# Queries and keys of a streaming-encoder layer: turned by VectorE and DMAs instead of TensorE

## The chip, the cores and the metric

The kernel runs on one core of a Trainium2 chip. The metric is device time in microseconds (us) of one execution; less is better. A core has five engines that run their own instruction queues side by side and wait for each other by semaphores: TensorE (matmuls, PE in the profile), VectorE (DVE), ScalarE (ACT), GpSimd (POOL) and SyncE (SP, which here only issues transfers). Transfers (DMA) are issued from the queues of SyncE, ScalarE and GpSimd. SBUF is the on-chip memory of 128 partitions; PSUM takes TensorE's results.

## The reference

One layer of depth 1 on 256 tokens of width 2048, in float32:

```
x += 1/2 * SwiGLU(RMSNorm(x))
h = RMSNorm(x);  [u | q | k | v] = h @ w_in          # u, q, k, v: 1024 columns each
y_ssm = GLU(S5(u))                                   # diagonal complex state space, scanned in time
q = rms_norm(q, q_norm);  k = rms_norm(k, k_norm)    # per head: 8 heads of 128, gain of 128 numbers
y_sb  = StickBreakingAttention(q, k, v)
x += concat(RMSNorm(y_ssm), RMSNorm(y_sb)) @ w_out
x += 1/2 * SwiGLU(RMSNorm(x))
x += RMSNorm((p @ w_ple_proj) * sigmoid(RMSNorm(x) @ w_ple_gate))
```

For the change the third and fourth lines matter. A head's query is q * rsqrt(mean(q*q) + eps) * q_norm, and the same for a key; the scores are q.k / sqrt(128) for each head. The scores' matmul contracts over the 128 numbers of a head, so both must lie with these numbers along the partitions, while the projection gives them with tokens along the partitions: they have to be turned.

## The kernel before

**Gemms.** Every large product is done in blocks of 512 columns. Weights come in quarters of 4 x 128 rows x 512 columns (1 MB, tile `raw`, three buffers, issued by SyncE). ScalarE casts each half of a quarter to a rounded part `whi` (L168), VectorE subtracts to get the rest `wlo` (L171); four buffers of each. TensorE does three products per tile, activation high x weight high (L292), low x high (L293), high x low (L297), into two of four accumulators `acc` in PSUM. A half quarter is one *step*: 12 matmuls. A cast can begin when the matmuls of four steps before have left its buffer.

**What sets the order.** The program is written as one stream of gemm steps. Other work hangs on it by `put_off(n, fn)`: `fn` is called n steps later, by `step()` after each half quarter. A recording layer then orders each engine's queue by its own costs; instructions that are pinned keep their place. On the chip each engine works its queue strictly in order, so an instruction that waits holds up all that stand behind it.

**The stage around the change.** After the first feed-forward part, `u_block` takes two blocks of u, then come four blocks: queries, keys, queries, keys (`qk_block`, L964), each 512 columns or four heads. Between their steps the state space runs in four groups q (`s5_main`): states (L843), rotation on VectorE (L860, L861), scan (L870), rotation back (L878 to L883), outputs on TensorE (L899), a copy (L919), a Gelu (L930) into `mid`. After the last Gelu `channels` (L945) moves the result into place by 32 small transfers `zt` on SyncE's queue, in between the loads of weights. Then come the blocks of v, the scores (`attn_scores`, L1009 to L1019), the gated unit (`glu`, L1144 to L1170) and the output projection.

**`qk_block` before.** Two scaled copies of the accumulators (L967), one square (L968), a reduction per head on VectorE (L970), a root in `rsqrt_mean` (L188 to L196), a product with it (L972). Five steps later TensorE turns the eight 128x128 pieces (`qk_turn`, L982) into PSUM, and a step after that ScalarE copies them to SBUF, scaled by the norm's gain, which lies along the partitions by then (`qk_scale`, L989).

**Turning by VectorE and DMAs.** Other tiles of the kernel are turned in another way: VectorE transposes the 32x32 blocks (`turn_blocks`, L203), and 16 transfers per tile carry the quarters of 32 partitions to their places (`turn_quarters`, L216).

**Row sums of the unit.** For the norm of y_ssm GpSimd adds the squares (L1090), TensorE sums them over partitions (`rms`, L1074), and a root follows. `glu` puts this off by 3 steps.

## Time and profile before

| | |
|---|---|
| median of 3 runs | 1879.85 us (1879.83 to 1881.18) |
| profiled execution | 1879.88 us |
| its span, first to last instruction | 1878.1 us |
| TensorE busy / VectorE / ScalarE / GpSimd | 1869.5 / 1184.8 / 963.8 / 50.3 us |
| granted TensorE clock | 1.000 |
| blocks of queries and keys, end of each on TensorE | 801.6, 828.5, 854.7, 879.6 us |

The profile gives start and length of instructions in us from the span's start, mean lengths in ns, and for idle time what ended it ("<-"). Matmuls overlap each other, so TensorE's busy time says little; the pitch from one step to the next is what to read. "q" behind an engine (SPq) means its queue, which issues transfers. L numbers are lines of the kernel before.

### The profile page before, as it was taken

What the parts mean: (1) busy time and instruction counts of PE and PEld (TensorE: products, weight loads), DVE (VectorE), ACT (ScalarE), POOL (GpSimd) and SP (SyncE); (2) the same over time, 40 slices, a digit from 0 to 9 for tenths busy, and PEclk for the clock granted to TensorE, in tenths of its full rate; (3) what the DMA queues carried; (4) which work ended last, traced back from release to release, by engine and by line L of the source; (5) the groups of instructions that cost most, each with busy time, mean ns of one, the idle gap of its engine ahead of it and who ended that gap; (6) DMA issues with size and microseconds to landing.
All of it is one profiled execution on the core that took longest, in us unless ns stands there. A gap on an engine that the chain in (4) does not pass through costs nothing.

```text
span 1878.1 us, 23877 instructions
## 1 busy us (share of the span) xinstructions
PE 1869.5 (100%) x9194; PEld 1549.5 (83%) x9194; DVE 1184.8 (63%) x1391; ACT 963.8 (51%) x1110; POOL 50.3 (3%) x84
## 2 busy tenths in 40 slices
PE   9999999999999999999999999999999999999998
PEld 7888888888888888888888888888888888888887
DVE  8867665444676776696566655455545566777655
ACT  7444444444455665455785544444444455666554
POOL 0011000000000000010020000000000000000000
PEclk9999999999999999999999999999999999999999
DMA  8788867766665667675646657666667665666563
GB/s 320 246 274 269 265 209 228 225 211 212 207 204 201 197 212 234 186 263 155 217 136 223 222 186 220 195 209 201 205 201 220 191 222 195 203 211 205 181 235 124
DMA packets 230387, 400.07 MB, mean 213 GB/s; under 512 B 26401, under 2 KB 50337, under 8 KB 229985
## 3 DMA queue, kind: packets, MB, share of 16 engines
q1 hardware_dynamic: 227824, 392.81, 65.2%
q0 software_dynamic: 1728, 4.33, 0.7%
q8 instruction: 72, 1.18, 0.3%
q10 hardware_dynamic: 720, 1.41, 0.2%
q14 instruction: 43, 0.34, 0.1%
HBM read 369.26 MB, written 9.83 MB: 202 GB/s over the span
## 4 chain that ended last, share of the span: by engine, by line
PE 97%; ACT 2%; DMA 0%; POOL 0%; issue 0%; SPq 0%; POOLq 0%
PE acc L292 32%; PE acc L297 32%; PE acc L293 32%; PE aux L899 0%; ACT whi L168 0%; DMA raw<-in_ffn_w_gate 0%; ACT nhi L178 0%; POOL sqg L1090 0%; PE aux L843 0%; PE aux L982 0%; PE aux L716 0%; ACT sg L1161 0%; PE aux L1015 0%; ACT L1161 0%; ACT L1034 0%
## 5 line engine op out<-in xcount | busy, mean ns | idle before, releaser
L171 DVE TENSOR_TENSOR wlo<-raw,whi 128x1024 fp32r<-128x1024 f32 x666 | 811.8, 1225 | 587.0 <-ACT whi L168 579.1
L168 ACT CAST whi<-raw 128x1024 fp32r<-128x1024 f32 x666 | 699.5, 1055 | 835.0 <-PE acc L293 776.2
L292 PE MATMUL acc<-whi,nhi 128*128 128x512 f32 x1568 | 613.5, 391 | 0.8 <-ACT whi L168 0.4
L293 PE MATMUL acc<-whi,nlo 128*128 128x512 f32 x1568 | 610.5, 389 | 0.0
L297 PE MATMUL acc<-wlo,nhi 128*128 128x512 f32 x1568 | 420.7, 389 | 0.0
L292 PE MATMUL acc<-whi,hhi 128*128 128x512 f32 x1056 | 410.8, 389 | 0.0
L293 PE MATMUL acc<-whi,hlo 128*128 128x512 f32 x1056 | 410.8, 389 | 0.0
L292 PEld LDWEIGHTS acc<-whi,nhi 128*128 128x128 f32 x1568 | 294.5, 188 | 63.9 <-ACT whi L260 1.3
L297 PEld LDWEIGHTS acc<-wlo,nhi 128*128 128x128 f32 x1568 | 294.3, 188 | 61.7 <-DVE wlo L171 0.4
L293 PEld LDWEIGHTS acc<-whi,nlo 128*128 128x128 f32 x1568 | 294.6, 188 | 60.3
L297 PE MATMUL acc<-wlo,hhi 128*128 128x512 f32 x1056 | 282.2, 389 | 0.0
L293 PEld LDWEIGHTS acc<-whi,hlo 128*128 128x128 f32 x1056 | 198.3, 188 | 41.2
L297 PEld LDWEIGHTS acc<-wlo,hhi 128*128 128x128 f32 x1056 | 198.2, 188 | 41.1
L292 PEld LDWEIGHTS acc<-whi,hhi 128*128 128x128 f32 x1056 | 198.2, 188 | 41.1
L171 DVE TENSOR_TENSOR hlo<-hT,hhi 128x1024 fp32r<-128x1024 f32 x88 | 107.2, 1219 | 0.0
L168 ACT CAST hhi<-hT 128x1024 fp32r<-128x1024 f32 x88 | 91.6, 1042 | 0.1
L464 DVE SCALAR_TENSOR_TENSOR h<-acc,sm,sg 128x512 f32<-128x512 f32 x44 | 31.0, 747 | 23.7 <-PE acc L297 23.7
L440 ACT ACTIVATE sg<-acc,sm 128x512 f32<-128x512 f32 x44 | 27.7, 681 | 6.8 <-PE acc L297 5.1
L203 DVE STREAM_TRANSPOSE mid<-h 128x512 f32<-128x512 f32 x44 | 28.6, 689 | 0.0
L829 POOL COPY dec<-rho 128x512 f32<-128x512 f32 x8 | 9.6, 1233 | 540.9 <-DVE hlo L171 441.6
L1322 POOL TENSOR_SCALAR sm<-sm,sm 128x1 f32<-128x1 f32 x1 | 0.3, 258 | 881.1 <-DVE sq L1315 881.1
L180 DVE SCALAR_TENSOR_TENSOR nlo<-h,gains,nhi 128x256 fp32r<-128x256 f32 x52 | 22.8, 489 | 1.2 <-ACT nhi L178 1.2
(251 smaller groups left out, 657.5 us busy)
## 6 DMA issues: line engine op xcount, KB each, us to landing
raw<-in_ffn_w_up SPq DMA_DIRECT2D x88, 1024.0 KB, 5.7
raw<-in_ffn_w_down SPq DMA_DIRECT2D x88, 1024.0 KB, 5.1
raw<-in_ffn_w_gate SPq DMA_DIRECT2D x86, 1024.0 KB, 5.2
raw<-in_w_in SPq DMA_DIRECT2D x32, 1024.0 KB, 5.7
raw<-in_w_out SPq DMA_DIRECT2D x16, 1024.0 KB, 5.3
raw<-in_w_ple_gate SPq DMA_DIRECT2D x16, 1024.0 KB, 5.4
hT<-mid SPq DMA_DIRECT2D x160, 64.0 KB, 4.9
h<-mid SPq DMA_DIRECT2D x176, 32.0 KB, 3.7
```

What stands on the lines that cost most here:

```text
L168: copy = nc.scalar.copy(hi, src)
L171: nc.vector.tensor_tensor(out=lo, in0=src, in1=hi.bitcast(F32), op=ALU.subtract)
L180: nc.vector.scalar_tensor_tensor(out=lo[:, j], in0=src[:, j], scalar=scale, in1=hi[:, j].bitcast(F32), op0=ALU.mult, op1=ALU.subtract,)
L203: nc.vector.transpose(mid[:, :, t, k0 : k0 + nk, :].rearrange("p q f b -> p f q b"), src.rearrange("p (f q b) -> p f q b", f=nk, q=4),)
L292: nc.tensor.matmul(ps[t], lhsT=lh, rhs=hi[:, j, cols], start=start and j == 0, stop=False)
L293: nc.tensor.matmul(ps[t], lhsT=ll, rhs=hi[:, j, cols], start=False, stop=False)
L297: nc.tensor.matmul(ps[t], lhsT=lh, rhs=lo[:, j, cols], start=False, stop=stop and j == 1)
L440: nc.scalar.activation(sg[:, t * NB : (t + 1) * NB], pg[t], AF.Silu, scale=xn.rs(t))
L464: nc.vector.scalar_tensor_tensor(out=hh[:, t * NB : (t + 1) * NB], in0=pu[t], scalar=xn.rs(t), in1=sg[:, t * NB : (t + 1) * NB], op0=ALU.m ...
L829: nc.gpsimd.tensor_copy(dvw[:, e], rho4[:, r0 : r0 + 4].unsqueeze(1).unsqueeze(3).to_broadcast([P, 2, 4, NC]))
L1322: pin(nc.gpsimd.tensor_scalar(total, square, 1.0 / D, ahead, op0=ALU.mult, op1=ALU.add))
```

## The change

Queries and keys are kept with tokens along the partitions until all their factors are in. The squares are taken per head straight from the accumulators, with their sums (eight small ones instead of two copies, a square and a reduction); the root is multiplied by the row's factor, eight small copies apply it, and a step later a product with the gain, now laid along the free dimension and loaded by two new transfers (`norms`), follows. Then VectorE turns the 32x32 blocks and 16 transfers on GpSimd's queue carry the quarters into place. TensorE's transposes and the scaled copies out of PSUM are gone. Queries come out in runs of 32 tokens, keys with a step of four numbers between tokens, so the operands of the scores are no longer contiguous. The first load of the kernel is two columns narrower. The row sums of the unit are put off by 4 steps instead of 3.

```diff
-    def turn_quarters(out, mid, steps):
+    def turn_quarters(out, mid, steps, queue=nc.sync):
...
-                    nc.sync.dma_start(
+                    queue.dma_start(
                         out[32 * q : 32 * q + 32].rearrange("p (t i w) -> p t i w", t=TT, i=4)[:, :, i],
-                        mid[32 * i : 32 * i + 32, q].rearrange("p t f b -> p t (f b)"),
+                        mid.rearrange("p (q t w) -> p q t w", q=4, t=TT)[32 * i : 32 * i + 32, q],
                     )
...
-    def qk_block(pool, dst, n, ps, xn, scale):
-        qs, sq = com("sg"), com("h")
+    def qk_block(pool, dst, n, ps, xn, weights):
+        heads = [(t, h, ps[t][:, h * DH : (h + 1) * DH]) for t in range(TT) for h in range(HB)]
+        ss = small(2 * HB)
+        for t, h, u in heads:
+            i = t * HB + h
+            nc.scalar.activation(com("sq")[:, :DH], u, AF.Square, scale=xn.rs(t), accum_out=ss[:, i : i + 1])
+        r = rsqrt_mean(ss, DH, 2 * HB)
         for t in range(TT):
-            nc.scalar.activation(qs[:, t * NB : (t + 1) * NB], ps[t], AF.Copy, scale=xn.rs(t))
-        nc.scalar.activation(sq, qs, AF.Square)
-        ss = small(2 * HB)
-        nc.vector.tensor_reduce(out=ss, in_=sq.rearrange("p (h d) -> p h d", d=DH), axis=AX.X, op=ALU.add)
-        r = rsqrt_mean(ss, DH, 2 * HB)
+            sl = slice(t * HB, (t + 1) * HB)
+            nc.vector.tensor_scalar(r[:, sl], r[:, sl], xn.rs(t), None, op0=ALU.mult)
+        qs = com("sg")
+        for t, h, u in heads:
+            i = t * HB + h
+            nc.scalar.activation(qs[:, i * DH : (i + 1) * DH], u, AF.Copy, scale=r[:, i : i + 1])
+        put_off(1, qk_turn, pool, dst, n, qs, weights)
+
+    def qk_turn(pool, dst, n, qs, weights):
+        each = qs.rearrange("p (h d) -> p h d", d=DH)
         nc.vector.tensor_tensor(
-            out=qs.rearrange("p (h d) -> p h d", d=DH), in0=qs.rearrange("p (h d) -> p h d", d=DH),
-            in1=r.unsqueeze(2).to_broadcast([P, 2 * HB, DH]), op=ALU.mult,
+            out=each, in0=each, in1=weights.unsqueeze(1).to_broadcast([P, 2 * HB, DH]), op=ALU.mult
         )
-        put_off(5, qk_turn, pool, dst, n, qs, scale)
-
-    def qk_turn(pool, dst, n, qs, scale):
-        pt = aux()
+        mid = com("h")
         for t in range(TT):
-            for h in range(HB):
-                pin(nc.tensor.transpose(
-                    pt[:, h * T + t * P : h * T + (t + 1) * P], qs[:, t * NB + h * DH : t * NB + (h + 1) * DH], ident
-                ))
-        put_off(1, qk_scale, pool, dst, n, pt, scale)
-
-    def qk_scale(pool, dst, n, pt, scale):
-        dst[n] = get(pool, f"{'q' if dst is qT else 'k'}{n}")
-        copy = nc.scalar.activation(dst[n], pt, AF.Copy, scale=scale)
-        if dst is kT and n == 1:
-            pin(copy)
+            turn_blocks(quartered(mid, "f b" if dst is qT else "b f"), qs[:, t * NB : (t + 1) * NB], t, 0, 4)
+        out = get(pool, f"{'q' if dst is qT else 'k'}{n}")
+        dst[n] = by_tile(out, HB) if dst is qT else out.rearrange("p (s h) -> p h s", h=HB)
+        turn_quarters(out, mid, 2, nc.gpsimd)
...
+                q, k = qT[n][:, h0 + j], kT[n][:, h0 + j]
                 pin(nc.tensor.matmul(
-                    ps[:, j * T : (j + 1) * T], lhsT=kT[n][:, hs : hs + P], rhs=qT[n][:, hs : hs + T],
-                    start=False, stop=True, skip_group_check=True,
+                    ps[:, j * T : (j + 1) * T], lhsT=k[:, :P], rhs=q, start=False, stop=True, skip_group_check=True
                 ))
...
-        return parts, rms(3, sq_acc, SW)
+        return parts, rms(4, sq_acc, SW)
...
-    q_scale = small(1)
-    nc.vector.tensor_scalar(q_scale, col("q_norm", 0), DH ** -0.5, None, op0=ALU.mult)
+    norms = get(mixp, "norms", 2 * DH)
+    for i, name in enumerate(("q_norm", "k_norm")):
+        nc.sync.dma_start(norms[:, i * DH : (i + 1) * DH], a[name][0].partition_broadcast(P))
+    nc.vector.tensor_scalar(norms[:, :DH], norms[:, :DH], DH ** -0.5, None, op0=ALU.mult)
```

More of the change, by code (lines that the diff above doesn't have):

```diff
@@ L28 @@
 SL = 4
-COLUMNS = ["ffn1_norm", "mix_norm", "ffn2_norm", "ple_norm", "out_norm_ssm", "out_norm_sb", "ssm_b_glu", "ssm_d",
-           "q_norm", "k_norm"]
+COLUMNS = ["ffn1_norm", "mix_norm", "ffn2_norm", "ple_norm", "out_norm_ssm", "out_norm_sb", "ssm_b_glu", "ssm_d"]
 @with_exitstack
@@ L152, in load_turned @@
         return turned
-    widths = [KD] * 4 + [NH] * 4 + [1] * 2
+    widths = [KD] * 4 + [NH] * 4
     NCOL = sum(widths)
@@ L206, in turn_blocks, with quartered @@
         )
-    def turn_quarters(out, mid, steps):
+    def quartered(mid, inner="f b"):
+        return mid.rearrange(f"p (q t {inner}) -> p q t f b", q=4, t=TT, b=32)
+    def turn_quarters(out, mid, steps, queue=nc.sync):
         def g():
@@ L363, in block @@
                     self.mid = com("mid")
-                mid = self.mid[:, n % 2 * 1024 : n % 2 * 1024 + 1024].rearrange(
-                    "p (q t f b) -> p q t f b", q=4, t=TT, b=32
-                )
+                mid = self.mid[:, n % 2 * 1024 : n % 2 * 1024 + 1024]
                 out = com("h")
                 for t in range(TT):
-                    turn_blocks(mid, xt[t][n], t, 0, 4)
+                    turn_blocks(quartered(mid), xt[t][n], t, 0, 4)
                 soon = n == ND - 1
@@ L421, in turned @@
             if f % 2 == 0:
-                mids[pair] = com("mid")[:, : 128 * TT * n_pair].rearrange(
-                    "p (q t f b) -> p q t f b", q=4, t=TT, b=32
-                )
+                mids[pair] = com("mid")[:, : 128 * TT * n_pair]
             for t in range(TT):
-                turn_blocks(mids[pair], hh[:, t * NB : (t + 1) * NB], t, f % 2 * 4, 4)
+                turn_blocks(quartered(mids[pair]), hh[:, t * NB : (t + 1) * NB], t, f % 2 * 4, 4)
             if f % 2 or f == NF - 1:
@@ L1013, in scores @@
             for j in range(2):
-                hs = (h0 + j) * T
+                q, k = qT[n][:, h0 + j], kT[n][:, h0 + j]
                 pin(nc.tensor.matmul(
-                    ps[:, j * T : (j + 1) * T], lhsT=kT[n][:, hs : hs + P], rhs=qT[n][:, hs : hs + T],
-                    start=False, stop=True, skip_group_check=True,
+                    ps[:, j * T : (j + 1) * T], lhsT=k[:, :P], rhs=q, start=False, stop=True, skip_group_check=True
                 ))
                 pin(nc.tensor.matmul(
-                    ps[:, NB + j * P : NB + (j + 1) * P], lhsT=kT[n][:, hs + P : hs + T],
-                    rhs=qT[n][:, hs + P : hs + T], start=False, stop=True, skip_group_check=True,
+                    ps[:, NB + j * P : NB + (j + 1) * P], lhsT=k[:, P:], rhs=q[:, 4:], start=False, stop=True,
+                    skip_group_check=True,
                 ))
@@ L1191, in layer_kernel @@
         u_block(pool, n, gemm_block(nm, w_in, n * NB, KD), nm)
-    q_scale = small(1)
-    nc.vector.tensor_scalar(q_scale, col("q_norm", 0), DH ** -0.5, None, op0=ALU.mult)
+    norms = get(mixp, "norms", 2 * DH)
+    for i, name in enumerate(("q_norm", "k_norm")):
+        nc.sync.dma_start(norms[:, i * DH : (i + 1) * DH], a[name][0].partition_broadcast(P))
+    nc.vector.tensor_scalar(norms[:, :DH], norms[:, :DH], DH ** -0.5, None, op0=ALU.mult)
     for n in range(2):
-        qk_block(mixp, qT, n, gemm_block(nm, w_in, q0 + n * NB, KD), nm, q_scale)
-        qk_block(mixp, kT, n, gemm_block(nm, w_in, k0 + n * NB, KD), nm, col("k_norm", 0))
+        qk_block(mixp, qT, n, gemm_block(nm, w_in, q0 + n * NB, KD), nm, norms[:, :DH])
+        qk_block(mixp, kT, n, gemm_block(nm, w_in, k0 + n * NB, KD), nm, norms[:, DH:])
     s5p.close()
@@ L1350 @@
 _INS = ["x", "not_ahead", "ffn1_w_gate", "ffn1_w_up", "ffn1_w_down", "w_in", "ssm_w_glu", "w_out", "ffn2_w_gate", "ffn2_w_up",
-        "ffn2_w_down", "w_ple_gate", "w_ple_proj", "ple_post_norm", "turned", "p_turned", "ssm_par",
+        "ffn2_w_down", "w_ple_gate", "w_ple_proj", "ple_post_norm", "q_norm", "k_norm", "turned", "p_turned", "ssm_par",
         "ssm_bc", "ssm_b_turned",
```

## The prediction

> **What bounds the kernel now.** I read the head of the page first, then the chain that ended last, then TensorE's waits, then time lines of the stage that the change touches (queries and keys are projected from 777 to 880 us).

> ```profile
> span 1878.1 us, 23877 instructions
> PE 1869.5 (100%) x9194; PEld 1549.5 (83%) x9194; DVE 1184.8 (63%) x1391; ACT 963.8 (51%) x1110; POOL 50.3 (3%) x84
> ...
> PE 97%; ACT 2%; DMA 0%; POOL 0%; issue 0%; SPq 0%; POOLq 0%
> ```
> ```profile
> PE aux L1074 <- POOL sqg L1090: 1.8, 1, 1.8
> ```
> TensorE is never free for long: 97% of the chain is its work. A microsecond counts only if it leaves TensorE's queue, or if it makes TensorE wait. The one wait worth naming is that of the unit's row sums (L1074) on GpSimd, 1.8 us.

> **Transposes leave TensorE.** The time line of TensorE around the third of the four groups of L982, and at the fourth:

> ```profile
> 872.08 1.07 PE L297 MATMUL acc<-wlo,nhi 128*128 128x512 f32 x4
> 872.99 1.03 PE L982 MATMUL aux<-ident,sg 128*128 128x128 f32 x8
> 873.78 0.47 PE L292 MATMUL acc<-whi,nhi 128*128 128x512 f32 x1
> ...
> 876.61 0.39 PE L292 MATMUL acc<-whi,nhi 128*128 128x512 f32 x1
> ...
> 879.33 0.39 PE L292 MATMUL acc<-whi,nhi 128*128 128x512 f32 x1
> ...
> 895.66 1.03 PE L982 MATMUL aux<-ident,sg 128*128 128x128 f32 x8
> 896.45 0.48 PE L292 MATMUL acc<-whi,nhi 128*128 128x512 f32 x1
> ```
> A step alone takes 879.33 - 876.61 = 2.72 us; with the transposes ahead of it 876.61 - 872.99 = 3.62. So a group costs 0.90 us and four cost 3.6 us. That is the most this part can give.

> **What ends TensorE's freedom there.** These rows are of ScalarE and SyncE just before the fourth group:

> ```profile
> 870.25 0.37 ACT L919 COPY yo<-aux 128x256 f32<-128x256 f32 x1 [1.87 <-PE aux L899]
> ...
> 871.93 0.60 ACT L930 ACTIVATE mid<-aux 128x512 f32<-128x512 f32 x1
> ...
> 894.62 2.00 ACT L168 CAST whi<-raw 128x1024 fp32r<-128x1024 f32 x2 [7.97 <-DMA raw<-in_w_in]
> ```
> ```profile
> 872.56 15.73 SPq L945 DMA_DIRECT2D zt<-mid  x24
> 888.39 0.52 SPq L282 DMA_DIRECT2D raw<-in_w_in  x1
> ```
> The last Gelu ends at 872.53. Behind it SyncE issues 24 small transfers of zt, and only then the weights whose cast starts at 894.62, 22.1 us after the Gelu. The first cast of the two is done about 895.67, 0.8 us before the step at 896.45 uses it. Today the fourth group of transposes fills just that hole. Without the four groups TensorE would be there at 895.66 - 2.7 = 892.9 and wait, unless the Gelu comes earlier too. The order of SyncE's queue is the same in the changed program, so this hangs on the Gelu, hence on ScalarE's and VectorE's queues in the third block (first block of queries, then keys, then queries).

> **ScalarE's part.** Rows of the operations removed, and those nearest to the added ones:

> ```profile
> L967 ACT ACTIVATE sg<-acc,sm 128x512 f32<-128x512 f32 x8 | 5.0, 682 | 5.3 <-PE acc L297 5.3
> L968 ACT ACTIVATE h<-sg 128x1024 f32<-128x1024 f32 x4 | 4.3, 1063 | 0.1
> L989 ACT ACTIVATE q<-aux,sm 128x1024 f32<-128x1024 f32 x2 | 2.2, 1119 | 2.4 <-PE aux L982 2.4
> L178 ACT ACTIVATE nhi<-aux,gains 128x256 fp32r<-128x256 f32 x12 | 4.7, 479 | 2.4 <-PE aux L1102 2.4
> L394 ACT ACTIVATION_READ_ACCUMULATOR sq<-x 128x1 f32 x32 | 6.0, 188 | 0.0
> 978.37 1.57 ACT L178 ACTIVATE nhi<-aux,gains 128x256 fp32r<-128x256 f32 x4 [2.44 <-PE aux L1102]
> ```
> Removed per block: two copies, a square, a scaled copy, 2 x 0.68 + 1.06 + 1.12 = 3.5 us. Added: eight squares and eight copies of 128x128 out of PSUM with a scale column. 256 to 512 columns costs 682 - 479 = 203 ns, so 128 columns cost about 479 - 102 = 0.38, and four in a row of 256 take 0.39 each, so 0.27 to 0.29 each for 128: eight copies 2.2 us. A square also reads its accumulator (0.19): 0.5 each, 4.0 us. ScalarE has 2.7 us more to do per block, and waits now in the middle: a copy needs the root, which VectorE works out.

> **VectorE's part.** The time line from the rotation of a block of states to the old product, without a gap between, the pitch of the small operations, and the load of the second block:

> ```profile
> 848.48 1.22 DVE L860 TENSOR_TENSOR rt<-aux,rot 128x1024 f32<-128x1024 f32 x1
> ...
> 863.90 0.17 DVE L193 TENSOR_TENSOR sm<-sm 128x8 f32<-128x8 f32 x1
> 864.10 0.17 DVE L194 TENSOR_TENSOR sm<-sm,sm 128x8 f32<-128x8 f32 x1
> ...
> 865.75 1.22 DVE L972 TENSOR_TENSOR sg<-sg,sm 128x1024 f32<-128x1024 f32 x1
> ```
> ```profile
> L970 DVE TENSOR_REDUCE sm<-h 128x8 f32<-128x1024 f32 x4 | 4.9, 1214 | 1.0 <-ACT h L968 1.0
> L203 DVE STREAM_TRANSPOSE mid<-h 128x512 f32<-128x512 f32 x44 | 28.6, 689 | 0.0
> ```
> ```profile
> 828.50:854.70 26.20, 26.20 (x266) 21.70 (x265) 22.94 (x28) 15.26 (x18) 3.20 (x4) 1.00 0.63 203
> ```
> Added: two small products (0.2 each at the pitch shown) and two turns, 0.4 + 1.4 us; removed: the reduction, 1.2 us; the product stays, now with the weights. VectorE is busy 22.94 of 26.2 us there, so lateness is not made up fast. In the new order the product and the turns of the keys stand ahead of the rotation at 848.48, in a hole of about 3 us that VectorE has now, so I keep that start at 848.4. From it to the first copy 17.3 - 1.2 + 0.4 = 16.5 us pass: the copies start near 865.0. ScalarE's order is then eight copies (2.2), two casts (2.0), copy, table, Gelu (2.3): Gelu done at 871.5, 1.0 us earlier than now, although its input from TensorE is 1.8 us earlier (two groups gone).

> Two unknown costs eat at this. The keys are turned into runs with a step of four floats. The nearest rows are products with strided and with plain operands:

> ```profile
> L586 DVE TENSOR_TENSOR s5s<-s5s x6: 184/185/189, 35.9 to 80.8; 128x32 f32<-128x32 f32 x6
> L586 DVE TENSOR_TENSOR s5s<-cft,s5s x6: 211/214/217, 82.4 to 85.1; 128x32 f32<-128x32 f32 x6
> ```
> 29 ns for 32 elements is 0.9 ns each; two turns of 512 give 0 to 0.9 us, I take 0.4 (the row steps farther). A gain is excluded: a turn moves the same elements. And the new quarters move 64 transfers of 32 KB through GpSimd's queue, 16 a block. The nearest rows are its transfers of coef, and weights in the same stretch (120 to 220 us):

> ```profile
> L672 POOL DMA_DIRECT2D coef<-scr_coef x32: 487/487/511, 130.4 to 211.1; - x32
> ...
> DMA to landing us min/median/max: 3.9/6.1/9.1
> ```
> ```profile
> raw<-in_ffn_w_gate SPq DMA_DIRECT2D x11, 1024.0 KB, 7.5
> ```
> Sixteen issues take 8 us, or some 16 with landings between, on an engine with nothing due: a block's quarters are there 16 us after its turn; the scores of the second half are put off by 16 steps (43 us) after the last block. GpSimd's next decays are queued behind the first block's quarters and are due about 20 us later; hidden, and if that cover were gone the scan would wait. The last block's quarters are in flight as the late weights land: landing took 6.2 (888.4 to 894.6), with such company elsewhere 7.5, so 0 to 1.3 us, below nothing excluded as bytes are added; I take 0.4, since a 32 KB piece each half microsecond is little beside the megabyte. [...]

> So the cast is done at 895.67 - 1.0 + 0.4 + 0.4 = 895.5 and the step starts then instead of at 896.45: of the 3.6 us some 0.9 is kept, 2.7 becomes a wait of TensorE on ScalarE's cast.

> **Scores.** Queries are read in runs of 32, keys as weights with a step of four floats: 4 loads for each of two lines in each of four groups, 32 in all.

> ```profile
> L1019 PEld LDWEIGHTS aux<-q,k 128*128 128x128 f32 x16 | 3.0, 190 | 0.4
> ...
> 899.94 0.38 PE L1019 MATMUL aux<-q,k 128*128 128x128 f32 x2
> 900.16 0.60 PE L1015 MATMUL aux<-q,k 128*128 128x256 f32 x2
> ```
> From below: 0, loads overlap matmuls, and a gain is excluded. From above by the strided row: 0.9 ns x 128 = 0.11 us each, 3.5 in all. A pair of L1019 takes 0.22, 0.11 a pass, so half of the loads have little to hide behind; I take half of 16 x 0.11, 0.8 us.

> **Row sums a step later.**

> ```profile
> 933.42 0.81 ACT L1027 ACTIVATE sp<-aux 128x768 f32<-128x768 f32 x1 [1.46 <-PE aux L1019]
> ```
> A step (2.72) now stands before the sums and covers their wait of 1.8 us, shown above, so 1.8 us is gained. The chain that ends in this wait runs through ScalarE from 933 us on; there ScalarE waits for the scores (1.46 us in the row), so the chain's start moves with TensorE. The root then comes 2.7 us later; the adds that need it follow six steps (16.3 us) after the unit, sums and root take about 11 + 5, and the banks they free are needed two steps later still: hidden.

> **Edits at nothing.**

> ```profile
> 688.21 16.69 SPq L282 DMA_DIRECT2D raw<-in_ffn_w_down  x4
> 709.97 11.25 SPq L282 DMA_DIRECT2D raw<-in_w_in  x3
> ```
> The two loads of weight rows and their small product stand between these two rows, where SyncE waits from 704.9 to 709.97 for a buffer; without that cover each issue would cost the queue about 0.5. Two columns less in the first load: no row shows a difference.

> **The sum.** The profiled execution took 1879.88 us (span 1878.1), and the median is 1879.85. 1879.9 - 0.9 - 1.8 + 0.8 = 1878.0.

> **Rivals.** First, the wait doesn't bind: if the Gelu comes 1.8 us sooner than I work out (VectorE catches up in its 3 us hole), all 3.6 is kept: 1879.9 - 3.6 - 1.8 + 0.4 (half of the strided loads' term) = 1874.9. For it speaks that TensorE's inputs move earlier by that much, against it VectorE's 88% load.
> Second, on the other side: the strided keys as weights. If a load took 0.40 instead of 0.19 with nothing to hide behind, 32 x 0.21 = 6.7 instead of 0.8: 1883.9. Slower than before from 2.7/32 = 0.08 us a load, by 0.2% from (2.7 + 3.8)/32 = 0.20. Against it: loads are hidden in every gemm row. [...]
> Third, ScalarE holds the Gelu up by 5 us more than worked out (each wait for a root keeps a cast behind it): about 1883.
> Fourth, the later sums wait as before and the late weights take all of the transposes: 1879.9.

> **How the numbers follow.** No change is told from one beyond about 0.2% (3.8 us). Partial gain 0.38 (own range 1876.2 to 1880.5); wait not binding 0.34; strided weights 0.13; ScalarE late 0.09; nothing moves 0.06. The likeliest gives 1878.0. Leaving out the far ends, 1874.3 to 1884.2. Faster: the 0.34 and 0.02 of the first. Same: the rest of the first and the fourth, 0.42. Slower 0.22.

> **What would show it.** TensorE without L982, its steps at 2.72; a wait of 2 to 3 us on L168 near 893; the last Gelu between 870 and 873; no wait at the sums; groups of the scores still 1.3 us. Wrong it is if the Gelu moves by more than 1.5 us, or the scores' loads show 0.4.

## The result, and the profile after

The changed kernel takes 1885.2 us (median; 1884.42 to 1886.18), the kernel before 1879.88 us beside it. The ratio is 1.0027, with a 95% interval from 1.0017 to 1.0037: slower by some 5 us, where I had forecast 1878.0 us and, at the far end, 1884.2. The profiled execution of the changed kernel took 1885.02 us, that of the kernel before 1879.88: a difference of 5.1 us, and it is this one that is taken apart below.

Line numbers in the changed kernel are some two lower than before: L167 casts the weights' high part, L170 makes the low part, L922 joins the scan's output, L928 is the Gelu, L943 sends zt, L294 to L299 are the large products, L1008 to L1017 the scores. The head of the changed kernel's page:

```profile
span 1883.2 us, 24019 instructions
PE 1870.1 (99%) x9162; PEld 1551.1 (82%) x9162; DVE 1188.5 (63%) x1403; ACT 968.9 (51%) x1190; POOL 85.3 (5%) x148
```

TensorE's busy time is not smaller than before (1869.5) although 32 transposes are gone, and it is now 99% of the span. Two of TensorE's waits in the changed kernel bear on the difference (of the 6.4 us, 0.4 stand at the kernel's start, as before):

```profile
PE acc L294 <- ACT whi L167: 6.4, 2, 6.0
PE acc L299 <- DVE wlo L170: 0.3, 1, 0.3
```

The wait for the row sums is gone, as forecast. In its place stands a wait of 6.0 us, at the late step where I expected 2.7. The time line of TensorE around it, first in the changed kernel, then the matching rows before (whose late step starts at 896.45, in the prediction):

```profile
892.37 1.07 PE L299 MATMUL acc<-wlo,nhi 128*128 128x512 f32 x4
899.46 0.80 PE L294 MATMUL acc<-whi,nhi 128*128 128x512 f32 x1 [6.02 <-ACT whi L167]
...
904.22 0.40 PE L1008 MATMUL aux<-late_r,ident_r 128*128 128x256 f32 x2
...
906.23 0.48 PE L294 MATMUL acc<-whi,nhi 128*128 128x512 f32 x1
...
909.07 0.40 PE L1008 MATMUL aux<-late_r,ident_r 128*128 128x256 f32 x2
```
```profile
899.27 0.40 PE L1009 MATMUL aux<-late_r,ident_r 128*128 128x256 f32 x2
...
900.74 0.47 PE L292 MATMUL acc<-whi,nhi 128*128 128x512 f32 x1
```

Two more things can be read there. The step behind the wait takes 904.22 - 899.46 = 4.76 us, before 899.27 - 896.45 = 2.82, while the next one takes 909.07 - 906.23 = 2.84 again. And a group of scores takes 906.23 - 904.22 = 2.01 us, before 900.74 - 899.27 = 1.47; the other three groups are longer by as much, 0.54 to 0.55 us. The cause of the slow step stands in the windows of the changed kernel (columns: window, length, busy time and instructions of PE, PEld, DVE, ACT and POOL, then the granted clock of TensorE as a mean over the window; the last two columns are of DMA):

```profile
896.00:897.00 1.00, 0.00 (x0) 0.00 (x0) 0.00 (x0) 0.00 (x0) 1.00 (x3) 0.89 1.06 393
900.00:903.00 3.00, 3.00 (x8) 2.31 (x7) 1.80 (x2) 0.35 (x1) 2.92 (x7) 0.50 0.85 272
903.00:904.00 1.00, 1.00 (x5) 0.78 (x4) 0.00 (x0) 0.00 (x0) 0.30 (x1) 0.70 1.03 373
```

The clock granted was halved while TensorE stood still. The windows next to the first row read 1.00 (893 to 896) and 0.50 (897 to 898); a mean of 0.89 over 1 us is 0.78 us at 1.00 and the rest at 0.50, so the clock fell at 896.78, 3.3 us after TensorE's last product had ended (892.37 + 1.07 = 893.44). The last row puts its return at 903.60 in the same way. It was at half rate for 6.8 us, the last 4.1 of them with the late step on TensorE. The scores' weight loads of the changed kernel are the other part:

```profile
L1017 PEld LDWEIGHTS aux<-q,k 128*128 128x128 f32 x16 | 4.5, 330 | 0.0
```

A load takes 330 ns in place of 190. So the 5.1 us are, in the order of the prediction: transposes -3.6, row sums -1.8, stall +6.0, slow step 4.76 - 2.82 = +1.9, four groups of scores 4 x 0.54 = +2.2, the wait at L170 +0.3: together +5.0.

Why did the weights come so late? Rows of SyncE, then of ScalarE, then of VectorE in the changed kernel:

```profile
875.95 16.24 SPq L943 DMA_DIRECT2D zt<-mid  x24
892.29 0.52 SPq L284 DMA_DIRECT2D raw<-in_w_in  x1
```
```profile
868.06 2.17 ACT L977 ACTIVATE sg<-acc,sm 128x128 f32<-128x128 f32 x8 [3.40 <-DVE sm L973]
...
875.32 0.60 ACT L928 ACTIVATE mid<-aux 128x512 f32<-128x512 f32 x1 [1.64 <-DVE aux L922]
...
898.36 1.99 ACT L167 CAST whi<-raw 128x1024 fp32r<-128x1024 f32 x2 [9.03 <-DMA raw<-in_w_in]
```
```profile
843.40 1.23 DVE L982 TENSOR_TENSOR sg<-sg,norms 128x1024 f32<-128x1024 f32 x1 [2.11 <-ACT sg L977]
...
845.68 2.03 DVE L202 STREAM_TRANSPOSE h<-sg 128x512 f32<-128x512 f32 x2
...
848.68 0.43 DVE L922 TENSOR_TENSOR aux<-aux,yo 128x256 f32<-128x256 f32 x1
850.71 1.23 DVE L170 TENSOR_TENSOR wlo<-raw,whi 128x1024 fp32r<-128x1024 f32 x1 [1.60 <-ACT whi L167]
851.85 1.22 DVE L858 TENSOR_TENSOR rt<-aux,rot 128x1024 f32<-128x1024 f32 x1
...
872.54 1.30 DVE L202 STREAM_TRANSPOSE h<-sg 128x512 f32<-128x512 f32 x2
```

And VectorE, then ScalarE, at the same place in the kernel before:

```profile
844.49 0.43 DVE L924 TENSOR_TENSOR aux<-aux,yo 128x256 f32<-128x256 f32 x1 [0.57 <-ACT yo L919]
847.34 1.23 DVE L171 TENSOR_TENSOR wlo<-raw,whi 128x1024 fp32r<-128x1024 f32 x1 [2.41 <-ACT whi L168]
```
```profile
844.48 1.28 ACT L930 ACT_TABLE_LOAD   x1
845.77 0.60 ACT L930 ACTIVATE mid<-aux 128x512 f32<-128x512 f32 x1
```

The hole that VectorE had before (2.41 us) stands behind its join (844.49), not ahead of it. What ends it is a chain on ScalarE: the Gelu needs the join, a cast stands behind the Gelu, and VectorE's next instruction waits for that cast. In the kernel before, the join was done at 844.92 and the load of the Gelu's table only at 845.76, so the join could have come 0.8 us later for nothing; the other 1.6 us of the hole follow the join wherever it goes. What the change adds, a wait of 2.11 us for ScalarE's copies and two turns, stands ahead of the join. So all but 0.8 us of the hole is not filled but pushed: join at 848.68 in place of 844.49, a hole of 1.60 us still there, rotation at 851.85 in place of 848.48. The Gelu now waits for the join (1.64 us at the last one). The last Gelu ends at 875.92 in place of 872.53, 3.4 us later, zt takes 16.24 us of SyncE's queue in place of 15.73, and the weights behind zt are asked for at 892.29 in place of 888.39.

### The profile page after: what moved, and what is told of

Its sections match the earlier page's. It is cut to its first block, busy times and chain, and to the rows that moved or that the text cites. A ratio compares the mean times of both kernels' runs of the same rounds, so it can differ in the third digit from the quotient of the medians.

```text
span 1883.2 us, 24019 instructions
## 1 busy us (share of the span) xinstructions
PE 1870.1 (99%) x9162; PEld 1551.1 (82%) x9162; DVE 1188.5 (63%) x1403; ACT 968.9 (51%) x1190; POOL 85.3 (5%) x148
## 4 chain that ended last, share of the span: by engine, by line
PE 97%; DVE 1%; ACT 1%; DMA 1%; issue 0%; SPq 0%; DVEq 0%; ACTq 0%
PE acc L294 31%; PE acc L295 31%; PE acc L299 31%; PE aux L897 0%; PE acc L1146 0%; PE acc L1151 0%; PE acc L1142 0%; DMA raw<-in_ffn_w_gate 0%; ACT whi L167 0%; DMA raw<-in_w_in 0%; PE aux L841 0%; DVE wlo L170 0%; PE aux L1014 0%; PE aux L1096 0%; PE aux L714 0%
## 5 line engine op out<-in xcount | busy, mean ns | idle before, releaser
L170 DVE TENSOR_TENSOR wlo<-raw,whi 128x1024 fp32r<-128x1024 f32 x666 | 811.2, 1224 | 583.0 <-ACT whi L167 578.3
L167 ACT CAST whi<-raw 128x1024 fp32r<-128x1024 f32 x666 | 696.4, 1052 | 818.3 <-PE acc L295 760.5
L294 PE MATMUL acc<-whi,nhi 128*128 128x512 f32 x1568 | 614.7, 392 | 6.8 <-ACT whi L167 6.4
L299 PE MATMUL acc<-wlo,nhi 128*128 128x512 f32 x1568 | 421.1, 390 | 0.3 <-DVE wlo L170 0.3
L294 PE MATMUL acc<-whi,hhi 128*128 128x512 f32 x1056 | 411.1, 389 | 0.0
L294 PEld LDWEIGHTS acc<-whi,nhi 128*128 128x128 f32 x1568 | 295.1, 188 | 70.3 <-ACT whi L167 7.6
L299 PEld LDWEIGHTS acc<-wlo,nhi 128*128 128x128 f32 x1568 | 294.8, 188 | 62.0 <-DVE wlo L170 0.7
L299 PE MATMUL acc<-wlo,hhi 128*128 128x512 f32 x1056 | 282.3, 389 | 0.0
L299 PEld LDWEIGHTS acc<-wlo,hhi 128*128 128x128 f32 x1056 | 198.3, 188 | 41.0
L294 PEld LDWEIGHTS acc<-whi,hhi 128*128 128x128 f32 x1056 | 198.3, 188 | 41.0
L170 DVE TENSOR_TENSOR hlo<-hT,hhi 128x1024 fp32r<-128x1024 f32 x88 | 107.1, 1218 | 0.0
L167 ACT CAST hhi<-hT 128x1024 fp32r<-128x1024 f32 x88 | 91.6, 1042 | 0.0
L202 DVE STREAM_TRANSPOSE mid<-h 128x512 f32<-128x512 f32 x44 | 28.6, 689 | 0.0
## 6 DMA issues: line engine op xcount, KB each, us to landing
raw<-in_ffn_w_up SPq DMA_DIRECT2D x88, 1024.0 KB, 5.7
raw<-in_ffn_w_down SPq DMA_DIRECT2D x88, 1024.0 KB, 5.1
raw<-in_ffn_w_gate SPq DMA_DIRECT2D x86, 1024.0 KB, 5.2
raw<-in_w_in SPq DMA_DIRECT2D x32, 1024.0 KB, 5.7
raw<-in_w_out SPq DMA_DIRECT2D x16, 1024.0 KB, 5.2
raw<-in_w_ple_gate SPq DMA_DIRECT2D x16, 1024.0 KB, 5.1
```

The lines of the kernel that those rows point to most:

```text
L167: copy = nc.scalar.copy(hi, src)
L170: nc.vector.tensor_tensor(out=lo, in0=src, in1=hi.bitcast(F32), op=ALU.subtract)
L202: nc.vector.transpose(mid[:, :, t, k0 : k0 + nk, :].rearrange("p q f b -> p f q b"), src.rearrange("p (f q b) -> p f q b", f=nk, q=4),)
L294: nc.tensor.matmul(ps[t], lhsT=lh, rhs=hi[:, j, cols], start=start and j == 0, stop=False)
L299: nc.tensor.matmul(ps[t], lhsT=lh, rhs=lo[:, j, cols], start=False, stop=stop and j == 1)
```

## The experiments

**The row sums alone, in the kernel before.**

```
-        return parts, rms(3, sq_acc, SW)
+        return parts, rms(4, sq_acc, SW)
```

> The kernel before with one edit: the row sums of the gated unit are taken one step later. Theory (the parts of the change add up: the sums gain what TensorE waited there, 1.8 us): 1879.9 - 1.8 = 1878.1, and no wait of TensorE for GpSimd's squares. Rival (the wait only moves to the next thing that needs the root of the sums, or the later sums hold up the output product): 1879.5 to 1880.5, with a new wait of 1 to 2 us behind 995 us.

Measured: 1878.04 us, ratio 0.9989 (0.9980 to 0.9998). The wait is gone, and none takes its place: in the window that held it TensorE is busy throughout (58.22 of 60 us before). The profiled execution was the slowest of the eleven (1879.79 us); in it TensorE stands still once more, for 1.3 us at L843 (823.25), for no cause that the trace shows and far ahead of the edit.

```profile
940.00:1000.00 60.00, 60.00 (x353) 53.46 (x352) 42.73 (x63) 47.09 (x73) 15.80 (x14) 1.00 0.46 158
```

The term of 1.8 us was right, and it is a gain by itself.

**zt asked for later, in the changed kernel.**

```
         def channels():
...
+            for _ in range(3):
+                yield
             for z in range(SL):
```

> The changed kernel with the first of the 32 transfers of zt asked for three steps later, so that on SyncE only twelve instead of 24 of them, some 8 us of issue, stand ahead of the late raw weights. Theory (the 6.0 us stall and the slow clock behind it, 4.76 - 2.82 = 1.94 us in one step, both come from SyncE's queue): no wait at the first late cast, granted clock 1.00 behind it, 1885.2 - 7.9 = 1877.3. Rival (ScalarE and VectorE are themselves late there, so that the cast comes late anyway): the wait shrinks to 2 to 4 us only, 1880 to 1883. Second rival (the gated unit then waits for zt, which is asked for later): a wait of some us at the gated unit, 1880 or more.

Measured: 1877.02 us, ratio to the kernel before 0.9985 (0.9976 to 0.9994); 8.2 us less than the changed kernel. SyncE, TensorE's waits, and one window:

```profile
876.27 9.14 SPq L945 DMA_DIRECT2D zt<-mid  x12
885.83 0.37 SPq L284 DMA_DIRECT2D raw<-in_w_in  x1
```
```profile
PE acc L294 <- ACT whi L167: 1.5, 2, 1.1
```
```profile
879.60:902.00 22.40, 22.40 (x102) 19.01 (x101) 12.13 (x18) 13.33 (x32) 9.11 (x18) 1.00 0.58 157
```

The Gelu is no earlier here (it starts at 875.65), yet the stall at the late step and the slow clock are gone; the 1.1 us of the row stand at a later step (915.32). Both rivals fall: VectorE's and ScalarE's lateness costs something only through the 24 transfers that SyncE puts between the Gelu and the weights, and the gated unit has the time for a later zt (no wait of TensorE there).

**The same edit in the kernel before.**

> The kernel before with its zt asked for three steps later, the same edit that took 8.2 us from the changed kernel. Theory (in the kernel before the late cast was done 0.8 us ahead of need, so earlier weights are worth nothing there but the 0.3 us wait at the next cast): 1879.6 to 1879.9. Rival (the edit is a gain by itself, and what it took from the changed kernel was not the stall): 1877 or less.

Measured: 1880.91 us, ratio 1.0001 (0.9992 to 1.0009); the median is 1 us above the range that I gave, the kernel before took 1880.37 beside it, and the ratio shows no change. The edit is worth nothing by itself. What it took from the changed kernel was the changed kernel's own stall.

**The keys side by side, in the changed kernel.** Each head's keys are contiguous; the transfers, twice as many for the keys, write runs of 32 numbers.

```
-            turn_blocks(quartered(mid, "f b" if dst is qT else "b f"), qs[:, t * NB : (t + 1) * NB], t, 0, 4)
+            turn_blocks(quartered(mid), qs[:, t * NB : (t + 1) * NB], t, 0, 4)
...
-        dst[n] = by_tile(out, HB) if dst is qT else out.rearrange("p (s h) -> p h s", h=HB)
+        dst[n] = by_tile(out, HB) if dst is qT else out.rearrange("p (h s) -> p h s", h=HB)
-        turn_quarters(out, mid, 2, nc.gpsimd)
+        turn_quarters(out, mid, 2, nc.gpsimd, dst is kT)
...
+                    to, of = out[32 * q : 32 * q + 32], mid[32 * i : 32 * i + 32]
+                    if apart:
+                        to = to.rearrange("p (f t i b) -> p t i f b", f=4, t=TT, i=4)[:, :, i]
+                        of = of.rearrange("p (q t f b) -> p q t f b", q=4, t=TT, f=4)[:, q]
+                        for t in range(TT):
+                            queue.dma_start(to[:, t], of[:, t])
+                        continue
```

> The changed kernel with each head's keys side by side in their tile, as in the kernel before: VectorE turns the keys as it turns the queries, and the transfers, twice as many for the keys, carry runs of 128 bytes. Theory (the score products are slow because their weight loads step over 16 bytes: 326 to 330 ns a load, 2.01 us a group of scores, against 190 ns and 1.47 us before): loads at 190 ns, four groups 0.54 us shorter, 1885.2 - 2.2 = 1883.0; VectorE's two turns of a key block 1.3 in place of 2.0 us, which shows at most as 0.7 us less stall. Rival (what slows the loads is something else about the keys' tile, or the score groups are hidden): loads unchanged or time unchanged, 1885.2. Against both: sixteen more transfers a key block could come late for the scores, a wait there and 1886 or more.

Measured: 1882.87 us, ratio to the kernel before 1.0016 (1.0007 to 1.0025), 2.3 us less than the changed kernel. The loads:

```profile
L1023 PEld LDWEIGHTS aux<-q,k 128*128 128x128 f32 x16 | 3.0, 189 | 0.4
```

The theory holds, and so does its small side: with keys turned as queries the last Gelu starts at 874.55, 0.77 us earlier, and the stall is 5.4 us.

**Strided keys alone, in the kernel before.** ScalarE's copy writes them interleaved.

```
-        copy = nc.scalar.activation(dst[n], pt, AF.Copy, scale=scale)
+        out = dst[n]
+        if dst is kT:
+            out, pt = out.rearrange("p (s h) -> p h s", h=HB), pt.rearrange("p (h s) -> p h s", h=HB)
+        copy = nc.scalar.activation(out, pt, AF.Copy, scale=scale)
...
+                k = kT[n].rearrange("p (s h) -> p h s", h=HB)[:, h0 + j]
...
-                    ps[:, j * T : (j + 1) * T], lhsT=kT[n][:, hs : hs + P], rhs=qT[n][:, hs : hs + T],
+                    ps[:, j * T : (j + 1) * T], lhsT=k[:, :P], rhs=qT[n][:, hs : hs + T],
```

> The kernel before with one edit: ScalarE's copy writes the turned keys with the four heads interleaved, as the changed kernel has them, and the score products take them so as weights. Theory: loads at 326 to 330 ns, each of four groups of scores 0.54 us longer, 1879.9 + 2.2 = 1882.1, and nothing else. Rival (the longer loads hide under the products of the stream, and the groups in the changed kernel are long for another reason): 1879.9. ScalarE's copy with a stride may take longer than 1.12 us; TensorE waits for none of it by either.

Measured: 1881.67 us, ratio 1.0009 (1.0000 to 1.0018): 1.8 us more, where 2.2 was expected; the lower end of the interval touches no change, so it is the rows that decide. The loads, and ScalarE's copy of the keys:

```profile
L1023 PEld LDWEIGHTS aux<-q,k 128*128 128x128 f32 x16 | 4.5, 329 | 0.0
...
L992 ACT ACTIVATE k<-aux,gains 128x1024 f32<-128x1024 f32 x2 | 4.2, 2106 | 2.1 <-PE aux L982 2.1
```

The same 329 ns (325 for the other line of loads) without anything else of the change. ScalarE's copy with that step takes 2.11 us in place of 1.12.

**What an idle of TensorE costs, in the kernel before.** The first four, or the first eight, of the zt transfers are sent twice, which delays the late weights by so much of SyncE's queue and changes nothing else. The diff is that of the first four; for eight, `< 1` is `< 2`.

```
-                    for r in range(4):
+                    for r in list(range(4)) * (2 if 2 * z + g < 1 else 1):
```

> The kernel before, with the first four of its transfers of zt asked for twice, so that four more of them (0.65 us each) stand on SyncE ahead of the late raw weights: these come 2.6 us later, and TensorE should stand still for 1.8 us at the late step (the cast was done 0.8 us before TensorE asked). Theory (an idle of that length costs its length alone, as the 1.8 us wait at the sums did): 1881.7, the clock granted at 1.00. Rival (any wait lowers the clock): 1882.5 or more, with the next step longer than 2.82 us.

> The same with the first eight asked for twice: the late raw weights 5.2 us later, TensorE idle 4.4 us. Theory (an idle of some length between 1.8 and 6.0 us halves the granted clock for some 3 to 4 us after): with the clock lowered, 1879.9 + 4.4 + 1 to 2 = 1885.3 to 1886.3, the first step after the idle 3.8 to 4.8 us; with the bound above 4.4 us, 1884.3 and a step of 2.82 us. Rival (the slow step in the changed kernel came from something else there, the strided keys or the transfers on GpSimd's queue): no slow step here, 1884.3.

Measured: 1882.86 us (ratio 1.0014, 1.0005 to 1.0023) and 1887.54 us (1.0046, 1.0031 to 1.0062; four executions). TensorE and its clock, with four more transfers, then with eight:

```profile
898.40 0.50 PE L292 MATMUL acc<-whi,nhi 128*128 128x512 f32 x1 [1.66 <-ACT whi L168]
901.27 0.40 PE L1009 MATMUL aux<-late_r,ident_r 128*128 128x256 f32 x2
```
```profile
897.00:900.00 3.00, 1.60 (x7) 1.34 (x8) 1.62 (x2) 2.70 (x3) 0.00 (x0) 1.00 0.39 60
```
```profile
901.20 0.80 PE L292 MATMUL acc<-whi,nhi 128*128 128x512 f32 x1 [4.70 <-ACT whi L168]
906.32 0.40 PE L1009 MATMUL aux<-late_r,ident_r 128*128 128x256 f32 x2
```
```profile
899.00:900.00 1.00, 0.00 (x0) 0.00 (x0) 0.00 (x0) 0.00 (x0) 0.00 (x0) 0.63 0.31 84
903.00:906.00 3.00, 3.00 (x8) 2.32 (x7) 0.54 (x1) 0.12 (x1) 0.00 (x0) 0.50 1.00 386
906.00:907.00 1.00, 1.00 (x7) 0.83 (x6) 0.00 (x0) 0.48 (x1) 0.00 (x0) 0.95 1.06 403
```

After 1.66 us of idle the step takes 901.27 - 898.40 = 2.87 us at a clock of 1.00. After 4.70 us it takes 906.32 - 901.20 = 5.12 us at 0.50, which is 2.3 us too long; the clock fell at 899.26, 2.8 us into the idle, and came back at 906.10, again 6.8 us later. That was more than I had expected (3.8 to 4.8 us), hence 1887.5 where I said at most 1886.3; the first missed too, by 1.2 us, though its profiled span (1880.3) is only 2.2 us longer than that of before, and what the rest is stays open. By its time alone the first met its rival's mark (1882.5 or more); by its rows, a step of 2.87 us at a clock of 1.00, it did not. So the rival for each falls: the slow step comes with the longer idle, and needs no strided keys and no transfers on GpSimd's queue. The clock stayed at 1.00 in this idle of 1.66 us, as in that of 1.78 us at the row sums of the kernel before, and fell to 0.50 in idles of 3.72 (below), 4.70 and 6.02 us; what a length between 1.78 and 3.72 us does, no run here shows. It was back at 1.00 after 4.1 us of work behind the idle of 6.02 us, after 4.9 behind that of 4.70, and after 6.1 behind that of 3.72.

**Products that nobody reads, in the changed kernel.** 24 products of ones into a bank that nobody reads are added to TensorE's work, meant for the idle of 6.0 us right ahead of the late step.

```
+    warm_up(24)
     for n in range(2):
         put_off(2, values, n, gemm_block(nm, w_in, v0 + n * NB, KD))
```

> [...] Theory (the slow step is the idle's doing, and no other part's): the raw weights come no earlier, so the late step starts where it did, but at the full clock: it takes 2.8 in place of 4.76 us, 1885.2 - 1.9 = 1883.3. Rival (the transfers or the strided keys slow it): the step stays at 4.8 us, 1885.2. Second rival (the products run over the end of the idle): later by what they run over.

Measured: 1883.43 us, 1.8 us less than the changed kernel, with useless products added. They do not stand where I had expected them, right ahead of the late step, but well ahead of that:

```profile
876.94 5.52 PE L237 MATMUL aux<-ones 128*128 128x128 f32 x48
...
899.69 0.50 PE L294 MATMUL acc<-whi,nhi 128*128 128x512 f32 x1 [0.90 <-ACT whi L167]
...
902.55 0.40 PE L1008 MATMUL aux<-late_r,ident_r 128*128 128x256 f32 x2
```
```profile
900.00:903.00 3.00, 3.00 (x15) 2.52 (x14) 2.03 (x2) 0.59 (x1) 2.95 (x7) 1.00 0.83 247
```

The next step of products starts at 882.22, 5.3 us later than without them (876.96), so TensorE comes that much later to the late step, and its idle there is 0.90 us in place of 6.02. The late step starts about where it did (899.69) and takes 2.86 us at a clock of 1.00. So the idle's price is 6.0 us and the clock's another 1.9, and the second goes away when other work keeps the idle short. What products inside the idle would do, no run here shows.

**ScalarE's copies left to VectorE, in the changed kernel.**

```
-            nc.scalar.activation(qs[:, i * DH : (i + 1) * DH], u, AF.Copy, scale=r[:, i : i + 1])
+            nc.vector.scalar_tensor_tensor(
+                out=qs[:, i * DH : (i + 1) * DH], in0=u, scalar=r[:, i : i + 1], in1=weights, op0=ALU.mult, op1=ALU.mult
+            )
...
-        nc.vector.tensor_tensor(
-            out=each, in0=each, in1=weights.unsqueeze(1).to_broadcast([P, 2 * HB, DH]), op=ALU.mult
-        )
```

> The changed kernel without ScalarE's eight copies a block: VectorE takes each head from the bank, times the root and the norm's weights in one instruction, eight of 128x128 in place of the wait and the one product of 1.23 us. Theory (the last Gelu came 3.4 us later than before because VectorE, in order, stood 2.1 us in each block for these copies): no idle of VectorE at that place, eight products of 0.20 to 0.25 us (1.6 to 2.0), so that a block takes VectorE 1.3 to 1.7 us less, the last Gelu at 872 to 874 in place of 875.3, the stall of 6.0 us down to 3 to 4.5, time 1880.5 to 1883.5, where the lower end needs the clock to stay up. Rival (the Gelu is late because of ScalarE's squares and their small reads, or VectorE's turns): the Gelu stays at 875, and the time at 1885.

Measured: 1883.11 us, ratio to the kernel before 1.0014 (1.0005 to 1.0023). VectorE, ScalarE, TensorE and its clock:

```profile
847.38 0.43 DVE L922 TENSOR_TENSOR aux<-aux,yo 128x256 f32<-128x256 f32 x1
```
```profile
872.74 0.60 ACT L928 ACTIVATE mid<-aux 128x512 f32<-128x512 f32 x1 [2.25 <-DVE aux L922]
```
```profile
897.21 0.80 PE L294 MATMUL acc<-whi,nhi 128*128 128x512 f32 x1 [3.72 <-ACT whi L167]
902.49 0.63 PE L1006 MATMUL aux<-late_r,ident_r 128*128 128x256 f32 x2
```
```profile
896.00:897.00 1.00, 0.00 (x0) 0.00 (x0) 0.00 (x0) 0.89 (x1) 0.47 (x1) 0.76 0.35 90
903.00:904.00 1.00, 1.00 (x6) 0.93 (x5) 0.00 (x0) 0.00 (x0) 0.00 (x0) 0.82 1.07 318
```

The join comes 1.3 us earlier in this block and 2.6 in the next (872.28 in place of 874.86), the last Gelu behind that one 2.6 us earlier too, and the stall is 2.3 us shorter. What VectorE saves ahead of its join is handed on to the Gelu in full, although ScalarE's squares are all still there. The Gelu is still 0.8 us later than in the kernel before; what part of that is the turns' and what the squares', no run here takes apart. The time falls by 2.1 us and no more, because after an idle of 3.72 us the clock is still halved, and for longer under the work: from 896.52 to 903.36, the same 6.8 us, of which the idle covers only the first 0.7. The step takes 902.49 - 897.21 = 5.28 us.

**Two and three edits together: a kernel that beats both.** The changed kernel with zt later and keys side by side, and then with ScalarE's copies left to VectorE as well.

> The changed kernel with both edits: zt asked for three steps later, and keys side by side in runs of 128 bytes. Theory (their gains are apart and add up): 1877.0 - 2.3 = 1874.7, no wait over 1 us at the late casts. Rival (twice the key transfers beside the later zt and raw transfers collide): 1876 to 1878, with a new wait at a score product or a cast.

> The changed kernel with three edits: zt asked for later, keys side by side, and VectorE's products straight from the banks in place of ScalarE's copies. Theory (TensorE no longer waits for anything in this stage, so an earlier Gelu buys nothing): 1875.3 as without the third edit, within 0.6. Rival (the waits of 0.5 and 0.4 us that are left at casts come from ScalarE's load): 1874.4.

Measured: 1875.32 us, ratio 0.9972 (0.9962 to 0.9983), and 1874.70 us, ratio 0.9971 (0.9960 to 0.9982). The waits of TensorE for these weights that are left, in the first and in the second; in each, 0.4 us stand at the kernel's start, as before, and 0.5 in the stage of queries and keys:

```profile
PE acc L300 <- ACT whi L167: 0.4, 1, 0.4
PE acc L305 <- DVE wlo L170: 0.5, 1, 0.5
```
```profile
PE acc L300 <- ACT whi L167: 0.9, 2, 0.5
```

The profiled spans are 1872.8 and 1872.9 us against 1878.1 before: 5.3 us, which is the 3.6 of the transposes and the 1.8 of the sums. The gains of the first two edits add up. The third brings nothing that can be told: 1874.70 lies between the theory's 1875.3 and the rival's 1874.4, the spans are the same, and so is the wait of 0.5 us.

## Why the prediction was wrong

- **Transposes, 3.6 us.** Right. With the stall and the strided loads mended, the spans differ by 3.6 + 1.8.
- **The wait for the late weights.** The place and the chain were right: Gelu, 24 transfers of zt, weights, cast. The size was wrong, 6.0 us where I had 2.7. The step that failed is "in a hole of about 3 us that VectorE has now, so I keep that start at 848.4": the rotation starts at 851.85. I took a hole for free time that the new work could use, without asking what ended it. It was ended by ScalarE's cast behind the Gelu, which needs VectorE's own join, and the new work stands ahead of that join; of the 2.41 us that it measured, 0.8 were free. VectorE's wait for ScalarE's copies, 2.11 us in that block, is a term that my list of its added work doesn't have at all. From the rotation to the copies my 16.5 us were good (851.85 to 868.06, 16.2). From the copies to the end of the Gelu I had 6.5 us and it took 7.9, by the same cause once more: the Gelu waits 1.64 us for the join. 3.1 + 1.4 us make the Gelu end at 875.92, not 871.5. My own mark for an error, a Gelu that moves by more than 1.5 us, was met.
- **The terms inside that step.** Squares with their reads (0.49 apart) and copies (2.17 for eight) were as worked out. The keys' turns cost 2.03 against 1.30 us, 0.73 more, in my range of 0 to 0.9, where I took 0.4. The weights took 6.1 us from issue to cast (6.2 before), so the 0.4 us for company on the DMA engines was not there.
- **Scores.** 2.2 us where I took 0.8; the range (0 to 3.5) held it. A load costs 0.14 us more, near my 0.11 from VectorE's row. What I mis-sized is how many of them show: of 32 x 0.14 = 4.5 us half shows, where I had let a quarter show. The second rival's longer loads are real, 330 ns against 190, at a third of its price of 6.7 us: the kernel before with nothing but strided keys loads in 329 ns, the changed kernel with keys side by side in 189.
- **Row sums, 1.8 us.** Right, alone and in the change.
- **The terms at nothing.** Right. GpSimd's 64 transfers take 0.53 us an issue, which is its 35 us more of busy time, and TensorE waits for none of them. The two loads of norm weights are issued at 704.84 and 705.38, and the next load of weights goes out at 709.85 (709.97 before).
- **The clock.** Not in the sum at all: +1.9 us. The page before shows no idle of TensorE longer than 1.8 us in the stages I read, so no row there could price it; the rows of a longer one are those above.
- **The sum redone.** 1879.9 - 3.6 - 1.8 + 6.0 + 0.3 + 2.2 = 1883.0, with the clock 1884.9; the profiled execution took 1885.0. The third rival (the Gelu 5 us later than worked out, 1883, 0.09) was the nearest to what happened, but its way was another: not casts that stay behind a root on ScalarE, but VectorE's join that stays behind a wait for ScalarE.

## What to carry to other kernels

Before you place new work in an engine's hole, find what ends the hole; if it is the answer to one of the engine's own later instructions, work put ahead of that instruction moves the hole instead of filling it (here all but 0.8 of 2.41 us). Where a late instruction releases a long row of transfers that stand in one queue ahead of the next weights, look at what its lateness does to them: here a Gelu 3.4 us late put the weights back by 3.9 us, and the cheapest cure was the order of that queue, worth 8.2 us. In this kernel idles of TensorE of 3.72, 4.70 and 6.02 us cost 2.5, 2.3 and 1.9 us beyond their length, and weights read with a step of 16 bytes cost 0.14 us a load, of which half showed: both belong in the sum.
